# Turning the convolved x with VectorE and DRAM instead of TensorE, two output groups taken ahead, and four pairs of heads in one visit, in a Mamba-2 and attention trunk

## The chip, the cores and the metric

One core of one Trainium2 chip runs the whole program. The metric is the device time of one execution in microseconds (us), as the median over several executions. TensorE (PE) multiplies matrices into PSUM, VectorE (DVE) and ScalarE (ACT) work elementwise, GpSimd (POOL) and SyncE (SP) here only issue DMAs.

## What is computed

The reference is a decoder trunk of two layers on one sequence of 256 rows and 2,048 columns, all in float32:

```python
h = rmsnorm(x, a_norm_g);  proj = h @ w_in                      # 2048 x 10304
z, xbc, dt = split(proj);  xbc = silu(causal_conv(xbc))         # 4 taps
xs, B, C = split(xbc);     dt = softplus(dt + dt_bias);  a = -dt*exp(A_log)
# per group g of 8 (8 heads of 64 columns each), one chunk of 256 rows:
cb    = C[g] @ B[g].T
y     = (cb * exp(a_cum[l] - a_cum[s]) for s <= l) @ (xs*dt) + D*xs
y     = grouped_rmsnorm(y * silu(z), gnorm_g);  x = x + y @ w_out
kv    = rmsnorm(x, kv_norm_g) @ w_kv                            # K with rope, V
q, z  = split(rmsnorm(x, b_norm_g) @ b_w_in)
o     = causal_softmax_attention(rope(q), K, V) * silu(z)       # 16 heads, one block of 256
x     = rmsnorm(x + o @ b_w_out, final_norm_g)
```

## The kernel before

**Blocks and units.** Every weight matrix is cut into blocks of 512 columns. A block is worked in units of two k tiles (256 rows of weights, 512 KB). A unit is one load on SP's queue (`load`, L292), a split of the float32 weights into a rounded part `hi` on ACT and the rest `lo` on DVE (`split`, L311), and twelve PE products of 128x128 by 128x512 (`products`, L343): for each half of the 256 rows and each k tile, x_hi by hi, x_lo by hi and x_hi by lo. The split of a unit stands three units ahead of its products (`LOOK = 3`, with four raw buffers and five hi/lo buffers). `ORDER` (L34) is the sequence of the blocks of the first layer: B, C, x and z are blocks of `w_in`, `o0` to `o3` take the output columns 0 to 3 over the k tiles 0 to 7 (groups 0, 1), `o10` to `o13` over the k tiles 8 to 15 (groups 2, 3), and `p0` to `p3` over the k tiles 16 to 31 (groups 4 to 7).

**Side work.** Everything else is written as generators (`conv_gen`, `cb_gen`, `pair_gen`, `norm_gen`, `z_gen`, `x1_gen`, `att_gen` and others). While the program is recorded, `Side.some` (L154) is called between products; it gives a generator its next step when the modelled end of its last step lies `MARGIN` = 750 ns behind the modelled PE. So the place of each side instruction in each engine's queue is fixed ahead of time by a table of costs, and nothing is reordered while the program runs: each engine works through its queue in order.

**A group of the SSD layer.** An x block gives 256 rows by 512 channels with rows on the partitions. `turn` (L376) brings it to channels on the partitions: DVE transposes 32x32 blocks (tile `T`), SP writes `T` to DRAM, POOL reads it back in four pieces as `U`. `conv_gen` (L621) then runs the four taps, the bias and silu with channels on the partitions (tile `xs`). For the y product the rows must be on the partitions again, so PE transposes `xs` 128x128 at a time, in two sets of four per group, into a PSUM bank `s`, and DVE multiplies each set by dt into `xd` (L646 to L659). `pair_gen` (L692) makes, for each pair of heads, the decay `em` (POOL reads the cumulated decay rows from DRAM, ACT takes differences and the exponential, DVE multiplies by `cb`), and at every second pair PE runs the y products of two pairs (tile `s<-em,xd`, in float32, which the profile records as sixteen records a visit). DVE then adds D xs from PSUM into a separate tile `yt` and multiplies by the gate. `norm_gen` (L745) scales the group into the operand `yn[g]`.

**The turn to the second layer.** `out_evac` (L867) adds each output block to the residual. After the last block of a column, `x1_gen` (L847) lets PE transpose the new residual, four k tiles per block column, and ACT and DVE split each into `kvop`, the operand of the K and V blocks that follow at once. `r1_gen` (L883) makes the row norm and the scaled rope table `csr`. `open_b` (L821) closes the first layer's buffers. In the second layer `att_gen` turns the attention weights through DRAM in the same way, and its outputs become `oop`, the operand of the last four blocks.

Only these lines set the order around the change:

```python
if entry[2] <= PE.ns - MARGIN:                  # L161, Side.some
    most -= self.advance(entry)
ks = range(8 * (i // 10), 8 * (i // 10) + 8) if kind == "o" else range(16, 32)   # L930
if u == first_p + 12:                           # L1202
    open_b()
```

## Time and profile before

| | us |
|---|---|
| median of three executions | 1143.38 (1142.94 to 1145.92) |
| the profiled execution, its own time | 1143.61 |
| its span, first to last instruction | 1141.9 |
| PE busy | 1130.1 (99% of the span) |
| DVE busy | 839.2 (73%) |
| ACT busy | 641.6 (56%) |
| moved by DMA | 258.91 MB, 227 GB/s on average |
| mean granted clock of TensorE | 0.997 of full speed |

Busy time of PE is an upper bound of its use, since products are pipelined and overlap in the records; starts of consecutive instructions tell what each costs. Stages: the SSD stage with all blocks up to `o13` ends at about 582 us, `p0` to `p3` at 674, K and V at 850, the second layer's input blocks at 1043. All side work is recorded by one helper, L126, so instructions are told apart by their tiles. An operation that reads a wide tile shows the tile's name without its number.

### The profile page before, as it was taken

The page shows a single profiled execution, that of the slowest core. Times are in us where ns is not written, and L with a number is a line of the kernel's source. Part 1 is how long each engine was busy: PE and PEld are TensorE (multiplying, and loading weights), DVE is VectorE, ACT ScalarE, POOL GpSimd, SP SyncE. Part 2 cuts the span into 40 slices and gives each one's busy share as a digit, 9 for nine tenths or more (in the row PEclk, how much of TensorE's full clock was granted, in tenths as well). Part 3 has the DMA queues.
Part 4 walks back from the last instruction along what each step waited for, and adds up shares of the span by engine and source line. Part 5 has one row for each costly group of instructions (what it writes and reads, how often), then busy time and mean ns, then how long its engine had stood idle before and what let it go on. Part 6 is the DMA issues. An engine that isn't in the chain of part 4 may idle for free.

```text
span 1141.9 us, 14900 instructions
## 1 busy us (share of the span) xinstructions
PE 1130.1 (99%) x5217; PEld 923.2 (81%) x5217; DVE 839.2 (73%) x1283; ACT 641.6 (56%) x890; POOL 124.4 (11%) x217
## 2 busy tenths in 40 slices
PE   9999999999999999999999999999999999999996
PEld 6888888888888888888878888888888888888885
DVE  5787878778799878787877558876445597887564
ACT  5666566767656666667554655434343444445353
POOL 2011112012011111101000000000000012122000
PEclk9999999999999999999999999999999999999998
DMA  8787888878778777777765467768658688888852
GB/s 263 222 242 242 249 229 278 268 243 253 210 222 240 223 237 225 237 234 231 215 232 177 162 197 218 224 200 261 220 174 244 209 248 237 263 250 261 254 185 92
DMA packets 130363, 258.91 MB, mean 227 GB/s; under 512 B 12976, under 2 KB 13824, under 8 KB 129904
## 3 DMA queue, kind: packets, MB, share of 16 engines
q1 hardware_dynamic: 119232, 226.01, 63.2%
q0 software_dynamic: 11056, 31.95, 10.9%
q8 instruction: 41, 0.67, 0.2%
q14 instruction: 34, 0.28, 0.1%
HBM read 235.83 MB, written 22.09 MB: 226 GB/s over the span
## 4 chain that ended last, share of the span: by engine, by line
PE 96%; DMA 1%; DVE 1%; ACT 0%; SPq 0%; issue 0%; ACTq 0%; DVEq 0%
PE ps L126 90%; PE s L126 6%; DMA raw<-in_a_w_in_dram 1%; PE ps_dt L126 0%; DVE xs L126 0%; DVE lo L126 0%; ACT hi L126 0%; SPq L416 0%; DVE x L126 0%; DVE T L126 0%; SPq L306 0%; ACT T L126 0%; ACT x L126 0%; DVE sfin L126 0%; ACTq L1243 0%
## 5 line engine op out<-in xcount | busy, mean ns | idle before, releaser
L126 DVE TENSOR_TENSOR lo<-raw,hi 128x1024 fp32r<-128x1024 f32 (+1 forms) x385 | 462.7, 1215 | 192.1 <-ACT hi L126 189.1
L126 ACT ACTIVATE hi<-raw 128x1024 fp32r<-128x1024 f32 (+1 forms) x385 | 397.7, 1052 | 263.3 <-PE ps L126 137.5
L126 PE MATMUL ps<-hi,hT 128*128 128x512 f32 x1280 | 401.1, 394 | 0.5 <-ACT hi L126 0.4
L126 PEld LDWEIGHTS ps<-hi,hT 128*128 128x128 f32 x1280 | 235.6, 188 | 49.2 <-issue 2.1
L126 PE MATMUL ps<-lo,hT 128*128 128x512 f32 x640 | 249.8, 390 | 0.0
L126 PE MATMUL ps<-hi,bop 128*128 128x512 f32 x512 | 161.1, 396 | 0.0
L126 PE MATMUL ps<-hi,yn 128*128 128x512 f32 x512 | 159.7, 393 | 0.0
L126 PE MATMUL ps<-hi,kvop 128*128 128x512 f32 x512 | 158.2, 390 | 0.0
L397 POOL DMA_DIRECT2D U<-turned x128 | 74.3, 587 | 748.9 <-DMA turned<-T 408.2
L126 PEld LDWEIGHTS ps<-lo,hT 128*128 128x128 f32 x640 | 120.1, 188 | 26.4 <-DVE lo L126 0.9
L126 PEld LDWEIGHTS ps<-hi,kvop 128*128 128x128 f32 x512 | 95.7, 188 | 19.7
L126 PEld LDWEIGHTS ps<-hi,bop 128*128 128x128 f32 x512 | 95.8, 188 | 19.4
L126 PEld LDWEIGHTS ps<-hi,yn 128*128 128x128 f32 x512 | 94.7, 188 | 19.4 <-issue 0.5
L126 PE MATMUL ps<-lo,yn 128*128 128x512 f32 x256 | 99.8, 390 | 0.0
L126 PE MATMUL ps<-lo,bop 128*128 128x512 f32 x256 | 99.8, 390 | 0.0
L126 PE MATMUL ps<-lo,kvop 128*128 128x512 f32 x256 | 99.7, 389 | 0.0
L126 PE MATMUL ps<-hi,oop 128*128 128x512 f32 x256 | 78.9, 390 | 0.0
L126 DVE STREAM_TRANSPOSE T<-ps 128x512 f32<-128x512 f32 x64 | 43.4, 699 | 25.6 <-ACT ps L126 15.9
L126 DVE SCALAR_TENSOR_TENSOR xs<-u,cw,xs 128x255 f32<-128x255 f32 (+2 forms) x144 | 59.7, 475 | 0.0
L126 ACT ACTIVATE em<-em,dal 128x128 f32<-128x128 f32 (+1 forms) x128 | 54.4, 449 | 5.0 <-DMA em<-AC 2.9
L126 PEld LDWEIGHTS ps<-lo,bop 128*128 128x128 f32 x256 | 48.0, 188 | 10.3
L126 PEld LDWEIGHTS ps<-lo,yn 128*128 128x128 f32 x256 | 48.0, 188 | 10.1
(165 smaller groups left out, 922.5 us busy)
## 6 DMA issues: line engine op xcount, KB each, us to landing
raw<-in_a_w_in_dram SPq DMA_DIRECT2D x159, 512.0 KB, 5.3
raw<-in_a_w_out_dram SPq DMA_DIRECT2D x64, 512.0 KB, 4.8
raw<-in_w_kv_dram SPq DMA_DIRECT2D x64, 512.0 KB, 4.8
raw<-in_b_w_in_dram SPq DMA_DIRECT2D x64, 512.0 KB, 4.7
turned<-T SPq DMA_DIRECT2D x64, 256.0 KB, 4.3
U<-turned POOLq DMA_DIRECT2D x128, 128.0 KB, 6.5
raw<-in_b_w_out_dram SPq DMA_DIRECT2D x32, 512.0 KB, 4.9
em<-AC POOLq DMA_DIRECT2D x32, 256.0 KB, 6.0
```

What stands on the lines that cost most here:

```text
L126: return call(out, *args, **kw)
L397: POOL.dma_start(U[32 * q:32 * q + 32].rearrange("p (b c) -> p b c", b=8), src)
```

## The change

- `conv_gen` no longer lets PE transpose `xs`. After silu, DVE transposes 32x32 blocks of `xs` into `u` (two instructions a group), SP writes `u` to DRAM (`turned_x`, 512 KB), POOL reads it back into `u` in four pieces of 128 KB, and DVE multiplies by dt into `xd` in four instructions from SBUF.
- `pair_gen` is split: `em_gen` makes the decays one pair at a time, and `y_gen` runs the y products of all four pairs of a group in one visit into two PSUM banks. It writes y over `xs`, so `yt` goes; `xs` and `em` get four buffers each.
- `p0` to `p3` keep the k tiles 24 to 31 alone; new blocks `o20` to `o23` take the k tiles 16 to 23 (groups 4, 5) just ahead of them.
- A generator whose next step needs a PSUM bank `s`, that is one that will use PE, waits until it lies 3,000 ns behind the modelled PE instead of 750.
- The factor 0.5 of the gate moves into a row norm `r0h` that is halved once, the gate product becomes two plain multiplications a group, and the second layer takes q2 ahead of z1.

```diff
+MARGIN_PE = 3000.0
-ORDER = "... z7 o12 o13 p0 p1 p2 p3".split()
+ORDER = "... z7 o12 o13 o20 o21 o22 o23 p0 p1 p2 p3".split()
-        entry[2] = max([at] + [e.ns for e, b in zip(self.engines, before) if e.ns > b])
+        entry[2] = max([entry[2], at] + [e.ns for e, b in zip(self.engines, before) if e.ns > b])
-            if entry[2] <= PE.ns - MARGIN:
+            if entry[2] <= PE.ns - (MARGIN_PE if getattr(entry[1], "pe", False) else MARGIN):
-... "xs": ([P, 4, L], 3), ... "em": ([P, 2, 384], 2), ... "yt": ([P, 4, L], 2)})]
+... "xs": ([P, 4, L], 4), ... "em": ([P, 2, 384], 4), ...})]
+        ready.pe = "s" in tags                                       # can()
-        late(blocks[n_out], 8, 2)
+        late(blocks[n_out], 4, 2)
+        DVE.tensor_scalar(r0h, r0, 0.5, None, op0=OP.mult)           # first_norm
...
+        U = u.rearrange("p j l -> p (j l)")                          # conv_gen
+        for t in range(2):
+            DVE.transpose(U.rearrange("p (b t j l) -> p t b j l", b=4, t=2, j=4)[:, t],
+                          v[:, :, t * P:(t + 1) * P].rearrange("p j (b l) -> p b j l", b=4))
+        X = hbm.tile([P, 1024], F32, name="turned_x", tag=f"X{group % 2}")
+        SP.dma_start(X, U)
+        written = DVE.ns + WRITE
+        for b in range(4):
+            src = bass.AP(tensor=X.tensor, offset=X.offset + b * L, ap=[[1024, 32], [32 * 1024, 4], [1, L]])
+            POOL.dma_start(U[32 * b:32 * b + 32].rearrange("p (a c) -> p a c", a=4), src)
+        yield copied(U, written, 4 * 600.0)
         yield lambda: "dal" in st and can("xd")()
-        for i in (0, 2):
-            yield can("s")
-            p = take("s").rearrange("p (t c) -> p t c", t=2)
-            for e in range(2):
-                for t in range(2):
-                    PE.transpose(p[:, t, e * P:(e + 1) * P], v[:, i + e, t * P:(t + 1) * P], ident)
-            yield
-            DVE.tensor_mul(xd[...], p..., st["dal"][...])
+        for t in range(2):
+            for h in range(2):
+                DVE.tensor_mul(xd[:, t]..., U..., st["dal"][...])
...
+    def y_gen(g):
+        yield lambda: ("xd", g) in st and st.get(("ems", g)) == 4
+        yield max(when["xd", g], *(when["em", g, j] for j in range(4)))
+        yield can("s", "s")
+        for i in (0, 2):
+            q = take("s").rearrange("p (j l) -> p j l", j=2)
+            for j in (i, i + 1):
+                ...                                  # the four y products of pair j, as before
+        for i in (0, 2):
+            yield
+            for j in (i, i + 1):
+                DVE.scalar_tensor_tensor(y[:, j, :], y[:, j, :], Dv[:, c:c + 1], Q[i // 2][:, j - i, :], ...)
+        yield lambda: ("z", g) in st
+        for i in (0, 2):
+            DVE.tensor_mul(v, v, by_channel(z)[:, i:i + 2])
+            yield
...
-            ks = ... if kind == "o" else range(16, 32)
+            ks = ... if kind == "o" else range(24, 32)
-    for kind, n in ("z0", "q0", "q1", "z1", "q2", "q3", "z2", "z3"):
+    for kind, n in ("z0", "q0", "q1", "q2", "z1", "q3", "z2", "z3"):
-        if u == first_p + 12:
+        if u == first_p + 4:
```

The products of the blocks are as many as before, 4,608 and the 16 of dt. What moves on the engines is shown at three places. The first is **PE at group 4**. Before, two sets of four transposes of `xs` stand among the products of a block (`ps<-hi,hT`, `ps<-lo,hT`), and a visit holds two pairs (each pair is one row of 64x256 and one of 64x128):

```order
L126 MATMUL ps<-lo,hT 128x512
L126 MATMUL s<-ident,xs 128x128 x4
L126 MATMUL ps<-hi,hT 128x512 x2
...
L126 MATMUL s<-em,xd 64x256 x2
L126 MATMUL s<-em,xd 64x128 x2
L126 MATMUL s<-em,xd 64x256 x2
L126 MATMUL s<-em,xd 64x128 x2
```

With the change the group's one visit stands between two blocks:

```order
L127 MATMUL ps<-lo,yn_2257 128x512
L127 MATMUL s<-em,xd 64x256 x2
L127 MATMUL s<-em,xd 64x128 x2
L127 MATMUL s<-em,xd 64x256 x2
L127 MATMUL s<-em,xd 64x128 x2
L127 MATMUL s<-em,xd 64x256 x2
L127 MATMUL s<-em,xd 64x128 x2
L127 MATMUL s<-em,xd 64x256 x2
L127 MATMUL s<-em,xd 64x128 x2
L127 MATMUL ps<-hi,hT 128x512 x2
```

The transposes are gone from PE in all eight groups, 64 of them, and sixteen visits of two pairs have become eight of four.

The second is **DVE at group 4**, where `lo` is the rest of one unit's weights, `nt` the norm of an earlier group, and `T<-ps` the turn of the next block. Before, `xd` is made from the PSUM tile of the transposes:

```order
L126 TENSOR_TENSOR xd<-s,dal 128x2x256
L126 TENSOR_TENSOR em<-em,cb 128x768
L126 TENSOR_TENSOR nt_3298<-nt_3298 128x2
L126 TENSOR_TENSOR lo<-raw,hi 128x1024
L126 TENSOR_TENSOR nt_3298<-nt_3298 128x2
L126 SCALAR_TENSOR_TENSOR nt_3298<-nt_3298 128x2
L126 TENSOR_TENSOR xd<-s,dal 128x2x256
```

With the change `u` is turned, and `xd` comes seven splits later:

```order
L127 STREAM_TRANSPOSE u<-xs 128x4x128 x2
L127 TENSOR_TENSOR lo<-raw,hi 128x1024 x2
L127 TENSOR_TENSOR em<-em,cb 128x768
L127 TENSOR_TENSOR lo<-raw,hi 128x1024
L127 TENSOR_TENSOR em<-em,cb 128x768
L127 TENSOR_TENSOR lo<-raw,hi 128x1024
L127 SCALAR_TENSOR_TENSOR z<-z,U 128x1024
L127 STREAM_TRANSPOSE T<-ps 128x512 x2
L127 TENSOR_TENSOR lo<-raw,hi 128x1024 x3
L127 TENSOR_TENSOR xd<-u,dal 128x4x64 x4
```

Between the turn of `u` and its first use stand seven splits here, and six or seven in the other groups; the trip through DRAM lies beside them.

The third is **DVE at the first K block**, whose operand `kvop` is made from PE's last transposes of the residual; `r` is the norm's chain, `csr` the scaled rope table, which needs PE's transposes of `r`. Before, the last `kvop` (k tile 15) stands two splits ahead of `csr`:

```order
L126 SCALAR_TENSOR_TENSOR kvop<-s,gv,kvop 128x256
L126 TENSOR_TENSOR r_6034<-r_6034 128x2
L126 SCALAR_TENSOR_TENSOR r_6034<-r_6034 128x2
L126 TENSOR_TENSOR lo<-raw,hi 128x1024
L126 TENSOR_SCALAR r1h<-r_6034 128x2
L126 TENSOR_TENSOR lo<-raw,hi 128x1024
L126 TENSOR_TENSOR csr<-cs,rB 128x512
```

With the change it stands behind `csr` and a pair of `x1T`:

```order
L127 TENSOR_TENSOR lo<-raw,hi 128x1024
L127 TENSOR_TENSOR csr<-cs,rB 128x512
L127 SCALAR_TENSOR_TENSOR x1T_5634<-x1T_5634,gv,rB 128x256 x2
L127 SCALAR_TENSOR_TENSOR kvop<-s,gv,kvop 128x256
L127 TENSOR_TENSOR bop_6123<-x1T_5634,bop_6123 128x2x256
```

On PE the transposes of `r` now come ahead of the last ones of `x`, with six products between them. From the transposes of `x` to the first product of the k tile 15 PE has nine products left, and from those of `r` fifteen.

## Rows read from the trace of the kernel before

**Rows 1.** The page, part 4: the chain of work that ended last, its shares of the span by engine and by line.

```profile
PE 96%; DMA 1%; DVE 1%; ACT 0%; SPq 0%; issue 0%; ACTq 0%; DVEq 0%
PE ps L126 90%; PE s L126 6%; DMA raw<-in_a_w_in_dram 1%; PE ps_dt L126 0%; DVE xs L126 0%; DVE lo L126 0%; ACT hi L126 0%; SPq L416 0%; DVE x L126 0%; DVE T L126 0%; SPq L306 0%; ACT T L126 0%; ACT x L126 0%; DVE sfin L126 0%; ACTq L1243 0%
```

**Rows 2.** The waits of PE, all that the profile lists: engine, tile, line <- what was waited for; us in total, times, the longest.

```profile
PE s L126 <- DVE early L126: 1.2, 1, 1.2
PE s L126 <- DMA xl<-in_x_dram: 0.5, 1, 0.5
PE ps L126 <- ACT hi L126: 0.4, 1, 0.4
```

**Rows 3.** The chain in order of time, one piece of it, 1,008 products long: start, us, what.

```profile
689.20 228.51 PE ps L126 x1008
```

**Rows 4.** Busy time by stretch of the span, the two stretches of the SSD stage: us from the start, length, busy us of PE, PEld, DVE, ACT, POOL (with instructions), granted clock of TensorE, DMA share, GB/s.

```profile
100.00:340.00 240.00, 240.00 (x1145) 195.30 (x1144) 190.57 (x297) 161.20 (x219) 31.98 (x52) 1.00 0.82 246
340.00:582.00 242.00, 242.00 (x1165) 196.36 (x1164) 198.25 (x313) 157.60 (x212) 31.19 (x51) 1.00 0.77 230
```

**Rows 5.** Groups of instructions of PE: shapes, count | busy us, mean ns of one.

```profile
L126 PE MATMUL s<-em,xd 128*64 128x256 f32 (+1 forms) x256 | 24.3, 332 | 0.0
L126 PE MATMUL s<-ident,xs 128*128 128x128 f32 x64 | 9.6, 272 | 0.0
```

**Rows 6.** PE in order of time around one set of four transposes of x: start, us from the first start to the last end, engine, line, instruction, count.

```profile
232.41 0.60 PE L126 MATMUL s<-ident,xs 128*128 128x128 f32 x4
232.76 0.71 PE L126 MATMUL ps<-hi,hT 128*128 128x512 f32 x2
233.31 0.40 PE L126 MATMUL ps<-lo,hT 128*128 128x512 f32 x1
233.54 0.62 PE L126 MATMUL ps<-hi,hT 128*128 128x512 f32 x2
```

**Rows 7.** PE in order of time around one visit of two pairs (columns as above). Six products lie between the third row shown and the last.

```profile
139.76 0.39 PE L126 MATMUL ps<-lo,hT 128*128 128x512 f32 x1
140.08 1.52 PE L126 MATMUL s<-em,xd 128*64 128x256 f32 x16
141.53 0.73 PE L126 MATMUL ps<-hi,hT 128*128 128x512 f32 x2
...
143.02 0.62 PE L126 MATMUL ps<-hi,hT 128*128 128x512 f32 x2
```

**Rows 8.** PE, two cuts into that same visit: the first begins at the fifth of its sixteen records, the second at the thirteenth, which does for the second pair what the fifth does for the first.

```profile
140.56 1.04 PE L126 MATMUL s<-em,xd 128*64 128x128 f32 x12
141.21 0.39 PE L126 MATMUL s<-em,xd 128*64 128x128 f32 x4
```

**Rows 9.** PE in order of time at the first C B products of a group (tile s<-xs).

```profile
98.98 0.39 PE L126 MATMUL ps<-lo,hT 128*128 128x512 f32 x1
99.48 0.92 PE L126 MATMUL s<-xs 128*128 128x256 f32 x4
```

**Rows 10.** Groups of instructions of DVE, by shape: count | busy us, mean ns of one | idle time before them and what ended it.

```profile
L126 DVE TENSOR_TENSOR lo<-raw,hi 128x1024 fp32r<-128x1024 f32 x383 | 461.3, 1218 | 191.5 <-ACT hi L126 188.5 <-PE ps L126 2.0
L126 DVE STREAM_TRANSPOSE T<-ps 128x512 f32<-128x512 f32 x64 | 43.4, 699 | 25.6 <-ACT ps L126 15.9 <-DMA turned<-T 5.0 <-PE ps L126 4.6
L126 DVE TENSOR_TENSOR xd<-s,dal 128x512 f32<-128x512 f32 x16 | 10.9, 683 | 0.1
L126 DVE SCALAR_TENSOR_TENSOR yt<-yt,z 128x256 f32<-128x256 f32 x32 | 13.1, 419 | 0.2
L126 DVE TENSOR_TENSOR x<-ps,x 128x512 f32<-128x512 f32 x32 | 21.5, 686 | 18.4 <-PE ps L126 18.4
```

**Rows 11.** One turn through DRAM in order of time: its two transposes on DVE, its four reads issued by POOL, and the first reader of what came back, on ACT. In brackets the idle time before and what ended it.

```profile
85.52 1.30 DVE L126 STREAM_TRANSPOSE T<-ps 128x512 f32<-128x512 f32 x2
92.05 2.32 POOL L397 DMA_DIRECT2D U<-turned  x4 [9.38 <-DMA turned<-T]
100.47 1.06 ACT L126 ACTIVATE u<-U 128x1024 f32<-128x1024 f32 x1 [2.49 <-DMA U<-turned]
```

**Rows 12.** The two longest waits of ACT (us in total, times, the longest), and two lines of DMA issues: count, KB each, median us from issue to landing.

```profile
ACT hi L126 <- PE ps L126: 137.5, 93, 3.0
ACT hi L126 <- DMA raw<-in_a_w_in_dram: 49.7, 30, 3.8
turned<-T SPq DMA_DIRECT2D x64, 256.0 KB, 4.3
U<-turned POOLq DMA_DIRECT2D x128, 128.0 KB, 6.5
```

**Rows 13.** The first K products, in order of time: a kvop half on DVE, the transposes of the norm on PE, the scaled table csr and a pair of x1T on DVE.

```profile
686.09 0.48 DVE L126 SCALAR_TENSOR_TENSOR kvop<-s,gv,kvop 128x256 fp32r<-128x256 f32 x1
688.82 0.38 PE L126 MATMUL s<-ident,r 128*128 128x128 f32 x2
690.31 0.68 DVE L126 TENSOR_TENSOR csr<-cs,rB 128x512 f32<-128x512 f32 x1
690.91 0.87 DVE L126 SCALAR_TENSOR_TENSOR x1T<-x1T,gv,rB 128x256 f32<-128x256 f32 x2
```

**Rows 14.** The last attention output, in order of time: the product that follows its visit on PE, and the end of its operand on DVE.

```profile
1065.58 0.70 PE L126 MATMUL ps<-hi,oop 128*128 128x512 f32 x2
1068.37 0.68 DVE L126 TENSOR_TENSOR oop<-U,oop 128x512 fp32r<-128x512 f32 x1
```

More of the change, by code (lines that the diff above doesn't have):

```diff
@@ L31 @@
 MARGIN = 750.0
-ORDER = "B0 d0 C0 x0 z0 x1 z1 x2 z2 x3 z3 B1 o0 C1 o1 x4 o2 z4 x5 o3 z5 x6 o10 z6 x7 o11 z7 o12 o13 p0 p1 p2 p3".split()
+MARGIN_PE = 3000.0
+ORDER = "B0 d0 C0 x0 z0 x1 z1 x2 z2 x3 z3 B1 o0 C1 o1 x4 o2 z4 x5 o3 z5 x6 o10 z6 x7 o11 z7 o12 o13 o20 o21 o22 o23 p0 p1 p2 p3".split()
 LOAD = 4700.0
@@ L224, in can, with ready @@
     def can(*tags):
-        return lambda: all(of(t).free(t) > 0 for t in tags)
+        def ready():
+            return all(of(t).free(t) >= tags.count(t) for t in tags)
+        ready.pe = "s" in tags
+        return ready
     def take(tag):
@@ L709, in pair_gen @@
         st["em", g, j], when["em", g, j] = E, clock.last
-        if j % 2:
-            yield lambda: ("xd", g) in st and ("em", g, j - 1) in st
-            yield max(when["xd", g], when["em", g, j - 1])
-            yield lambda: of("s").free("s") > 1 and (("y", g) in st or can("yt")())
-            for i in (j - 1, j):
-                xd, E, q = st["xd", g], st.pop(("em", g, i)), take("s")[:, :L]
+        st["ems", g] = st.get(("ems", g), 0) + 1
+        if st["ems", g] == 4:
+            give(st["cb", g])
@@ L724, in pair_gen @@
-            if ("y", g) not in st:
-                st["y", g], st["n", g] = take("yt"), 0
+        give(xd)
+        for i in (0, 2):
             yield
-        else:
-            yield lambda: ("q", g, j) in st
-            yield when["q", g, j]
-        xd, xs, q = st["xd", g], st["xs", g], st.pop(("q", g, j))
-        y = st["y", g][:, j, :]
-        DVE.scalar_tensor_tensor(y, xs[:, j, :], Dv[:, c:c + 1], q, op0=OP.mult, op1=OP.add)
-        give(q)
-        st["x", g] = st.get(("x", g), 0) + 1
@@ L741, in pair_gen @@
-        st["n", g] += 1
-        if st["n", g] == 4 and g not in (1, 3):
+        for i in (0, 2):
+            v = y[:, i:i + 2, :].rearrange("p j (b l) -> p j b l", l=32)
+            DVE.tensor_mul(v, v, by_channel(z)[:, i:i + 2])
+            yield
+        st["y", g] = y
+        st["n", g] = 4
+        if g not in (1, 3):
             give(z)
@@ L791, in z_gen @@
             z = take("z")
-        ACT.activation(z, U, AF.Tanh, scale=0.5)
+        ACT.activation(z, U, AF.Tanh)
         yield
@@ L799, in evac @@
         def evac(ps, t):
-            U, there = turn(ps, t, r0)
+            U, there = turn(ps, t, r0h)
             if t:
@@ L812, in evac @@
             for j in range(4):
-                side.add(pair_gen(g, j), lambda: "AC" in st and can("em")())
+                side.add(em_gen(g, j), lambda: "AC" in st and can("em")())
+            side.add(y_gen(g))
             side.add(norm_gen(g), lambda: st.get(("n", g)) == 4)
@@ L929, in trunk_kernel @@
             n = i % 10
-            ks = range(8 * (i // 10), 8 * (i // 10) + 8) if kind == "o" else range(16, 32)
+            ks = range(8 * (i // 10), 8 * (i // 10) + 8) if kind == "o" else range(24, 32)
             if name == "p0":
@@ L1048, in att_gen @@
         yield
-        if ("z", h0) not in st:
+        if ("gate", h0) not in st:
             yield can("q")
@@ L1054, in att_gen @@
             o = z
-            yield lambda: ("z", h0) in st
-        gate = st.pop(("z", h0))
+            yield lambda: ("gate", h0) in st
+        gate = st.pop(("gate", h0))
         DVE.tensor_mul(gate.heads, in_32s(o), gate.heads)
@@ L1082, in gate_gen @@
         for i, half in enumerate(two(U)):
-            st["z", 4 * n + 2 * i] = half
+            st["gate", 4 * n + 2 * i] = half
     def zb_evac(n):
```

41 lines of the change are left out of this document (22 added, 19 removed).

## The prediction

> **What bounds it.** I read the chain of work that ended last first. PE carries 96% of it: 90% products of weight blocks (`ps`) and 6% side work (`s`) [rows 1]. Then the waits of PE: three in the whole span, 2.1 us together, all at the start [rows 2]. So PE hardly ever stands still, and the time is the sum of what its instructions cost. A product costs what the longest clean piece of the chain shows: 228.51 us for 1,008, that is 0.227 us [rows 3]. The 4,624 products of both kernels take 1,048 us at that price, and the rest of PE's time is mostly side visits. The other engines have room even in the SSD stage: in 482 us DVE is busy 389 us (81%) and the 16 DMA engines 0.77 to 0.82, at a full clock [rows 4]. ACT waits longer for PE to free a split buffer (137.5 us) than for weights of the first layer (49.7 us) [rows 12], which says that the splits run ahead of PE as far as their buffers let them. A PE instruction that goes is therefore worth its own cost, as long as nothing new makes PE wait.
>
> **The transposes of x.** Sixty-four leave PE [rows 5]. Their busy time of 9.6 us is not their price, since records overlap, so I take starts. Four start at 232.41, three products follow, and the next one starts at 233.54: 1.13 us, of which three products are 0.68 [rows 6]. A set costs 0.45 us, and sixteen sets 7.2 us. All of it lies on PE's path.
>
> **Four pairs a visit.** The y products stay, the switches between products and side work halve. After the product at 139.76 the next would have started at 139.99; the visit and six products end at 143.02. That is 3.03 us, less 6 x 0.227 = 1.36: a visit of two pairs costs 1.67 us [rows 7]. Inside it the second pair follows the first by 141.21 - 140.56 = 0.65 us [rows 8]. Two pairs are 1.30, so entering and leaving costs 0.37. Eight visits fewer give 8 x 0.37 = 3.0 us. The least that it can give is nothing, if two pairs that now share a PSUM bank hold each other up. I take 3.0: the step of 0.65 that I measured crosses from one bank to another, and the four products of a pair share a bank already and fill that step between them.
>
> **The wider margin.** There is almost nothing for it to win, because PE does not wait for its side operands [rows 2]. One place is visible: before the first C B products PE starts 0.50 us after its last product instead of 0.23 [rows 9]. With the change they stand one split later in its queue, so I count 0.3 us won. Elsewhere I count nothing.
>
> **What is added.** On DVE a group gets two transposes (0.70 each, as `T`, which reads PSUM), and four multiplications of 256 elements (0.42, as the gate's) take the place of two of 512 (0.68); the gate goes the other way, from four of 0.42 to two of 0.68. That is 1.4 us a group, 11.2 in all, and `o20` to `o23` bring eight more additions of 0.69, 5.5 us [rows 10]. These 17 us cost nothing while DVE keeps a fifth of its time free; that cover gone, each would delay a split. The halved norm is one instruction on two columns a partition. DMA gets 8 x 2 x 512 KB = 8.4 MB on 258.9, which at 238 GB/s, the mean of the two stretches, is 7% of what the SSD stage moves: its share goes from 0.80 to about 0.86. On SP the write of `turned_x` stands between weight loads and waits for DVE's transposes, on POOL its reads wait for that write; behind them wait weight loads for units further ahead on SP, and the reads of z and of `em` on POOL.
>
> **The trip through DRAM** is the one new wait on DVE: `xd` stands there with splits queued behind it. The same kind of trip now runs from the end of `T` at 86.82 to the arrival at 100.47, 13.7 us [rows 11]. Six or seven splits stand between, one per unit of 12 x 0.227 = 2.72 us, so at least 16.3 us. I count nothing; at worst PE waits when the splits' lead of three units, 8.2 us, is gone too, which takes a trip of 24.5 us. The Trainium skill (VectorE: DVE Perf Modes, The three transpose paths) says that a plain copy whose access pattern does the transposing is 19 times slower than the hardware's transpose when the innermost stride is large, and it sends a 128x128 transpose to TensorE. That speaks against this change; the rows are on the other side, since reads of this kind land in 6.5 us [rows 12] and each piece they move is a contiguous run.
>
> **Output blocks and second layer.** No product is added or removed. PE waited neither at `p0` nor in the attention, so the longer cover of group 7 and the other order of q2 and z1 win nothing [rows 2]. Two places get tighter. At the first K block the last `kvop` is made behind `csr`: `csr` begins 1.49 us after PE's transposes of the norm (a split lies in between, as it does with the change), then come 0.68, 0.87 and 0.48, 3.5 us [rows 13]. PE has 15 products and two visits of two transposes, about half of 0.45 each, until it reads it: 3.9 us. If that split starts late by all its 1.22 us, PE waits 0.8; so the place costs 0 to 0.8, and I take 0.3. The last attention output now has 21 products, 4.8 us, from its visit to its use; now it takes from 1065.58 to 1069.05, 3.5 us [rows 14]. Nothing.
>
> **Sum.** -7.2 - 3.0 - 0.3 + 0.3 = -10.2 us on the profiled execution's 1143.61, that is 1133.4; the median of the runs is 0.23 us lower, so I forecast **1133.2 us**.
>
> **Rivals.** First, *the tight places take a part back*: the joined visit saves nothing (+3.0), and a split of 1.22 stands late at both tight places (+2.4): 1138.6 us. For it: four decays and two banks must now be ready at once, and both places have under 1.5 us in hand. Against it: em and xs have twice and four thirds the buffers, and the margin is four times as wide.
>
> Second, *the weights become the bound*. If the DMA engines can't pass the 0.82 that the busiest stretch shows [rows 4], the SSD stage must grow by 0.86/0.82, some 5% of 482 us, 24 us; if half of the 8.4 MB finds gaps, 12 us, which eats the gain: 1145 us, no change. Against it: the waits for weights are a third of the waits for PE.
>
> Third, on the other side, *the trip is late*. DVE stands at `xd`, the splits behind it are late, and PE waits once a group. From 24.5 us on each microsecond costs eight; it is slower than before by more than 0.3% from 24.5 + (10.2 + 3.4)/8 = 26.2 us on, twice the 13.7 of the rows, and a trip of 28 us gives 8 x 3.5 - 10.2 = +18: 1161 us. For it: two kinds of trip now share POOL's queue, where one write that is late holds all reads behind it. Against it: 13.7 us included a POOL that had waited 9.38 us for the write alone [rows 11]. By the skill's factor of 19 this rival would be the forecast; no row bears that factor out.
>
> **How the numbers follow.** The forecast has a chance of 0.78, the first rival 0.13, the second 0.05, the third 0.04. About 0.3%, 3.4 us, can be told from no change, so faster means below 1140.0. The first two cases are faster, 0.91; the second rival is no change, 0.05; the third slower, 0.04. The range runs from 1131.5 (the sum without the K block's 0.3 is 1132.9, and the runs of before scatter by more than a microsecond around their median) to 1139.5, which takes in a joined visit without gain, the K block at 0.8 and the first rival with a microsecond of scatter.
>
> **What would show it.** Right: no `s<-ident,xs` on PE; the y products in eight visits of thirty-two records, each costing 1.67 + 1.30, about 2.97 us; `s` at about 5% of the chain; PE's waits still under some 3 us; DVE busy some 856 us; 267 MB moved. Wrong: waits of PE for `lo`, `kvop` or `oop`; DVE waiting for `u<-turned_x` by more than a few us a group; a lower granted clock.

## The result, and the profile after

| | before | forecast | after |
|---|---|---|---|
| median, us | 1143.89 (1142.94 to 1145.92) | 1133.2 (1131.5 to 1139.5) | 1158.76 (1156.22 to 1163.08) |
| profiled execution, us | 1143.61 | 1133.4 | 1159.48 |
| DVE busy, us | 839.2 | 856 | 850.4 |
| moved by DMA, MB | 258.91 | 267 | 267.29 |

The ratio of after to before is 1.0131, with an interval of 1.0097 to 1.0166: slower by 15 us (before was run beside it), where I had given faster 0.91. The work went as forecast: no `s<-ident,xs` is left, and a visit of four pairs costs what the sum said. This is PE around one that nothing disturbs, columns as in rows 7; five products lie between its second and third row:

```profile
418.71 0.39 PE L127 MATMUL ps<-lo,yn 128*128 128x512 f32 x1
419.03 2.82 PE L127 MATMUL s<-em,xd 128*64 128x256 f32 x32
...
423.04 0.39 PE L127 MATMUL ps<-lo,hT 128*128 128x512 f32 x1
```

423.04 - 418.71 - 6 x 0.227 = 2.97 us, as forecast. But PE, which had stood still for 2.1 us [rows 2], now does so for 18.8 us in all, where I had given under 3. The chain by engine and line (to [rows 1]) shows how much of the end is set elsewhere:

```profile
PE 53%; DVE 16%; DMA 15%; ACT 9%; issue 6%; POOL 1%; ACTq 0%; SPq 0%; DVEq 0%; POOLq 0%
PE ps L127 49%; DVE lo L127 7%; DMA raw<-in_a_w_in_dram 6%; ACT hi L127 5%; PE s L127 4%; DVE xs L127 3%; DMA raw<-in_w_kv_dram 2%; DMA turned<-T 2%; DMA Es<-turned_E 2%; DMA raw<-in_a_w_out_dram 1%; DVE T L127 1%; ACT em L127 1%; DMA U<-turned 1%; ACT xs L127 1%; ACT u L127 1%
```

The longest waits of PE (to [rows 2]):

```profile
PE s L127 <- issue: 4.2, 2, 2.8
PE s L127 <- DMA Es<-turned_E: 3.7, 2, 2.7
PE ps L127 <- DVE lo L127: 2.2, 4, 0.7
PE s L127 <- DVE r L127: 1.9, 1, 1.9
PE s L127 <- DVE nt L127: 1.9, 3, 0.8
PE ps L127 <- DVE kvop L127: 1.8, 1, 1.8
```

To have one measure for all kernels I took every start-to-start step of PE, subtracted what that pair of instructions takes when nothing waits, and added up what is over by more than 0.06 us. It takes in waits and the slow clock behind them. It is read from the one profiled execution of each kernel, which lies up to 6 us from its median (1164.76 and 1158.68 us in the run without `o20` to `o23`), and a sum falls up to 3.4 us short of what that execution's time asks for. So a difference of 2 or 3 us between two kernels says little. **Lost time of PE by stretch**, us (the stretch limits are those of the profile before; in the slower kernels the stages end later than that):

| kernel | 100 to 582 (SSD) | 582 to 674 (p blocks) | 674 to 850 (K, V) | from 850 |
|---|---|---|---|---|
| before | 0.1 | 0 | 0 | 1.4 |
| after | 11.0 | 2.4 | 5.3 | 7.0 |

That is 24.2 us more than before; with the 10.2 saved and the 15.9 by which the profiled execution is longer, 26.1 were to be found, and some 2 us lie in steps too small to be counted.

**In the SSD stage** the two windows of [rows 4] read after the change:

```profile
100.00:340.00 240.00, 233.34 (x1093) 187.84 (x1094) 192.73 (x303) 157.95 (x218) 39.54 (x66) 0.99 0.88 257
340.00:582.00 242.00, 241.01 (x1129) 197.18 (x1127) 192.20 (x298) 159.13 (x217) 36.71 (x60) 1.00 0.83 247
```

The place of the first y visit shows what happens. Windows of before, same columns:

```profile
136.00:142.00 6.00, 6.00 (x39) 4.53 (x38) 4.16 (x7) 1.83 (x2) 2.80 (x5) 1.00 0.91 252
142.00:148.00 6.00, 6.00 (x28) 4.94 (x27) 3.03 (x4) 1.76 (x2) 0.94 (x2) 1.00 1.03 265
148.00:152.00 4.00, 4.00 (x19) 3.32 (x18) 0.54 (x1) 3.97 (x7) 0.00 (x0) 1.00 0.59 216
```

and of after, with one more behind it:

```profile
136.00:142.00 6.00, 6.00 (x28) 4.99 (x27) 5.42 (x7) 2.35 (x3) 2.20 (x4) 1.00 1.02 340
142.00:148.00 6.00, 4.98 (x22) 3.78 (x21) 0.73 (x1) 0.99 (x1) 2.33 (x4) 1.00 1.05 228
148.00:152.00 4.00, 2.24 (x16) 1.66 (x18) 3.70 (x6) 1.12 (x2) 0.51 (x1) 0.87 0.97 230
...
151.00:155.00 4.00, 4.00 (x27) 3.08 (x24) 0.80 (x1) 1.06 (x2) 2.17 (x3) 0.58 0.89 249
```

The DMA share, 0.82 on average, touched 1.03 here before the change too; now it is about 1 for sixteen us, with the four reads of `turned_x` (issued from 136.84 on) among weight loads and a turn. What suffers is the landing of the weights. The weight loads of 125 to 150 us (count, KB, median us to landing), first before, then after:

```profile
raw<-in_a_w_in_dram SPq DMA_DIRECT2D x9, 512.0 KB, 6.6
```

```profile
raw<-in_a_w_in_dram SPq DMA_DIRECT2D x8, 512.0 KB, 9.1
```

So a split is late, and with it everything behind it on DVE. ACT, DVE and PE of after, in order of time, an extract of each (five products lie between the last two rows of PE):

```profile
147.01 1.06 ACT L127 ACTIVATE hi<-raw 128x1024 fp32r<-128x1024 f32 x1 [5.54 <-PE ps L127]
```

```profile
148.10 1.23 DVE L127 TENSOR_TENSOR lo<-raw,hi 128x1024 fp32r<-128x1024 f32 x1 [5.37 <-ACT hi L127]
149.24 1.43 DVE L127 TENSOR_TENSOR xd<-u,dal 128x256 f32<-128x256 f32 x4
```

```profile
146.60 0.39 PE L127 MATMUL ps<-lo,hT 128*128 128x512 f32 x1
149.76 5.03 PE L127 MATMUL s<-em,xd 128*64 128x256 f32 x32 [2.78 <-issue]
...
155.98 0.40 PE L127 MATMUL ps<-lo,hT 128*128 128x512 f32 x1
```

`u` was there, its last read having landed at 146.79; `xd` is late because the split ahead of it on DVE is. The profile puts ACT's idle time down to PE and PE's to "issue", the last releasers that it saw. The load of the weights that ACT splits at 147.01 tells more. It was issued at 135.34 and landed 11.6 us later, at 146.91. In a run with the same order and small transfers, told below, the same load was issued at 135.69 and took 6.4 us, and PE did not stop. The two loads (count, KB, us to landing), first after, then that run:

```profile
raw<-in_a_w_in_dram SPq DMA_DIRECT2D x1, 512.0 KB, 11.6
```

```profile
raw<-in_a_w_in_dram SPq DMA_DIRECT2D x1, 512.0 KB, 6.4
```

The visit then runs for most of its length at the lower of TensorE's two clocks, 1.2 GHz instead of 2.4 (granted clock 0.58 on average from 151 to 155 us, last window row).

**The trip itself** takes longer than the prediction's 13.7 us, and the place of `xd` is nearer than its 16.3. From the traces, us by group of the SSD layer, from the end of the turn of `u` on DVE to the landing of the last read, and to the first `xd`:

| group | 0 | 1 | 2 | 3 | 4 | 5 | 6 | 7 |
|---|---|---|---|---|---|---|---|---|
| after, trip | 14.9 | 20.1 | 15.0 | 16.8 | 15.1 | 18.2 | 17.5 | 19.0 |
| after, to `xd` | 17.4 | 20.7 | 16.7 | 19.1 | 15.3 | 18.8 | 17.7 | 19.2 |
| same order, small transfers, to `xd` | 12.3 | 20.7 | 14.8 | 17.0 | 13.7 | 17.6 | 15.0 | 16.4 |

With small transfers nothing on DVE waits for `u`, so the last row is about the room that the order gives. The trip of after is longer than that in groups 0, 2 and 4 to 7. At the first y visit a split in time would have brought `xd` forward by no more than 2.4 us, since `u` would then have held it until 146.79. The wait of DVE for `u` in all, and its longest, in group 6 (the turn of `u` and `xd`), after:

```profile
DVE xd L127 <- DMA u<-turned_x: 4.3, 3, 2.6
```

```profile
515.58 1.30 DVE L127 STREAM_TRANSPOSE u<-xs 128x512 f32<-128x512 f32 x2
...
534.55 1.43 DVE L127 TENSOR_TENSOR xd<-u,dal 128x256 f32<-128x256 f32 x4 [2.58 <-DMA u<-turned_x]
```

and the same two in the run with small transfers:

```profile
507.62 1.30 DVE L127 STREAM_TRANSPOSE u<-xs 128x512 f32<-128x512 f32 x2
...
523.89 1.43 DVE L127 TENSOR_TENSOR xd<-u,dal 128x256 f32<-128x256 f32 x4
```

**At the first K block** `r` itself is late, and `kvop` behind a split that is late too. DVE of after, to [rows 13]:

```profile
693.71 0.16 DVE L127 TENSOR_REDUCE r<-ss 128x2 f32<-128x8 f32 x1 [1.06 <-ACT T L127]
...
701.39 1.23 DVE L127 TENSOR_TENSOR lo<-raw,hi 128x1024 fp32r<-128x1024 f32 x1 [1.40 <-ACT hi L127]
702.53 0.69 DVE L127 TENSOR_TENSOR csr<-cs,rB 128x512 f32<-128x512 f32 x1
703.14 0.88 DVE L127 SCALAR_TENSOR_TENSOR x1T<-x1T,gv,rB 128x256 f32<-128x256 f32 x2
703.93 0.48 DVE L127 SCALAR_TENSOR_TENSOR kvop<-s,gv,kvop 128x256 fp32r<-128x256 f32 x1
```

PE transposes `r` at 698.38 after a wait of 1.9 us; `csr` follows 4.15 us later, not 1.49.

### The profile page after: what moved, and what is told of

It is laid out like the page before. It is cut to its first block, busy times and chain, and to the rows that moved or that the text cites. A ratio compares the mean times of both kernels' runs of the same rounds, so it can differ in the third digit from the quotient of the medians.

```text
span 1157.8 us, 14848 instructions
## 1 busy us (share of the span) xinstructions
PE 1129.2 (98%) x5153; PEld 920.1 (79%) x5153; DVE 850.4 (73%) x1308; ACT 638.6 (55%) x889; POOL 142.9 (12%) x249
## 2 busy tenths in 40 slices
DMA packets 133050, 267.29 MB, mean 231 GB/s; under 512 B 13616, under 2 KB 14464, under 8 KB 132592
## 4 chain that ended last, share of the span: by engine, by line
PE 53%; DVE 16%; DMA 15%; ACT 9%; issue 6%; POOL 1%; ACTq 0%; SPq 0%; DVEq 0%; POOLq 0%
PE ps L127 49%; DVE lo L127 7%; DMA raw<-in_a_w_in_dram 6%; ACT hi L127 5%; PE s L127 4%; DVE xs L127 3%; DMA raw<-in_w_kv_dram 2%; DMA turned<-T 2%; DMA Es<-turned_E 2%; DMA raw<-in_a_w_out_dram 1%; DVE T L127 1%; ACT em L127 1%; DMA U<-turned 1%; ACT xs L127 1%; ACT u L127 1%
## 5 line engine op out<-in xcount | busy, mean ns | idle before, releaser
L127 PEld LDWEIGHTS ps<-lo,kvop 128*128 128x128 f32 x256 | 48.1, 188 | 11.1 <-DVE lo L127 1.1
L127 PEld LDWEIGHTS ps<-hi,oop 128*128 128x128 f32 x256 | 48.6, 191 | 10.0
```

What stands on the lines that cost most here:

```text
L127: return call(out, *args, **kw)
```

## The experiments

The four figures in brackets behind each result are the lost time by stretch, in the order of the columns of the table above. Each ratio is to the kernel before, run beside it.

### Single parts put back into the changed kernel

```diff
-MARGIN_PE = 3000.0
+MARGIN_PE = 750.0
```

> The changed kernel with one number put back: steps that need a PSUM bank s wait for 750 ns behind the modelled PE again, not 3,000. The trace of the changed kernel (1158.8 us) shows PE waiting at some twenty places. Theory M (the wider margin puts PE's side steps too near to, or past, the products that need their results): the waits for r and kvop at the first K block (2.1 + 1.9 us) and for Es in the attention (1.2 + 2.8 us, and about 3 us of half clock behind the second) go, some 11 us, so about 1148 us. Theory X (the trip of x through DRAM is what makes weights, splits and decays late): these waits lie in the SSD stage, about 16 us there with the half clock at 150 us, and stay; with the second layer as it is, 1157 to 1161 us. Theory O (the shorter p blocks and the order of the second layer's blocks make those places tight, whatever the margin): 1157 to 1161 us as well.

1157.94 us, ratio 1.0123 (1.0100 to 1.0145) [7.6, 0.6, 7.3, 6.3]. Not clearly faster: theory M alone falls. PE no longer waits for `kvop`, but it waits 3.2 us for the residual at the transposes of x.

```diff
 # conv_gen: the lines of before again, four transposes by PE into s, xd from s; give(u) after silu
-        SP.dma_start(X, U)
+                    PE.transpose(p[:, t, e * P:(e + 1) * P], v[:, i + e, t * P:(t + 1) * P], ident)
```

> The changed kernel with PE's 64 transposes of x back and the trip of x through DRAM gone; margin, blocks, joined visits and the rest as in the changed kernel. The transposes cost PE 7.2 us (16 sets of 0.45). Theory X: some 16 us of waits and half clock in the SSD stage go with the trip, so 1158.8 + 7.2 - 16 = 1150 us, and the DMA share between 100 and 340 us falls from 0.88 to about 0.82. Theory M or O alone: the SSD stage's waits stay, 1158.8 + 7.2 = 1166 us. With both halves true it is between 1150 and 1156 us.

1154.10 us, ratio 1.0082 (1.0067 to 1.0098) [2.2, 0, 5.4, 4.6]. PE works 7.2 us more, and the program is 0.0049 of the time, 5.6 us, shorter than with the whole change: here the trip cost more than it gave. The intervals of the two ratios just touch, so the 5.6 can be anything from 1 to 10 us, and the order is drawn anew. The DMA share between 100 and 340 us is 0.83, as forecast, and the losses from K on stay.

```diff
-... o12 o13 o20 o21 o22 o23 p0 p1 p2 p3
+... o12 o13 p0 p1 p2 p3          # p over range(16, 32), late(..., 8, 2), first_p + 12
```

> The changed kernel without the blocks o20 to o23: p0 to p3 take the k tiles 16 to 31 again, with eight units each. Theory O: the waits for r and kvop at the first K block, 2.1 + 1.9 us, go, because the transposes of the residual have eight units a block instead of four; group 7 has less cover, but before that was enough: about 1154.5 us, and 8 additions fewer on DVE. Theory M: the two waits stay, since the margin sets them: 1158 to 1160 us. Theory X says nothing of these places: 1158 to 1160 us.

1158.68 us, ratio 1.0129 (1.0112 to 1.0145) [15.7, 7.6, 1.2, 5.3]. The waits for `r` and `kvop` are gone, as theory O said, but PE now waits for `yn` of group 7, and the SSD stage, whose order is drawn anew, loses more, so the forecast of 1154.5 us failed.

```diff
-"z0", "q0", "q1", "q2", "z1", "q3", "z2", "z3"
+"z0", "q0", "q1", "z1", "q2", "q3", "z2", "z3"
```

> The changed kernel with the second layer's blocks in their old order (z1 ahead of q2). Theory O: the wait for Es at 1054 us (2.8 us) and the 3 us of half clock behind it go, perhaps the 1.2 us at 998 us too: 1152 to 1153 us. Theory M: the margin, not the order, makes the attention's last steps late, and a wait of the same kind stays: 1157 to 1160 us.

1160.84 us, ratio 1.0145 (1.0117 to 1.0174) [13.7, 1.1, 8.1, 5.1]. No gain; PE does not wait for `Es`, but for `oop` (1.6 us, with slow clock behind).

### Single parts on the kernel before

The parts of change are the ones shown in the diff of the change; each stands alone here.

> The kernel before with one part of the change: x is turned by VectorE and through DRAM, PE's 64 transposes of it go; visits of two pairs, margin, blocks and order as before. Theory X (the trip makes weights, splits and decays late): 7.2 us are saved on PE and some 16 us of waits and half clock come in the SSD stage, 1152 to 1154 us, with PE waits for lo, hi, em, nt or squares between 100 and 582 us and none behind. Theory N (the trip is hidden, as the prediction had it, and the loss needs the other parts): 1136 to 1138 us.

1192.78 us, ratio 1.0423 (1.0396 to 1.0450) [38.0, 18.3, 0, 1.4]. Far worse than either theory. PE around `yn` of group 3:

```profile
288.37 1.55 PE L126 MATMUL s<-em,xd 128*64 128x256 f32 x8 [4.34 <-DVE xs L126]
295.75 0.66 PE L126 MATMUL s<-ident,nt 128*128 128x128 f32 x2 [5.83 <-DVE nt L126]
307.66 1.55 PE L126 MATMUL s<-em,xd 128*64 128x256 f32 x8 [11.25 <-DVE em L126]
310.20 1.55 PE L126 MATMUL s<-em,xd 128*64 128x256 f32 x8 [0.99 <-PE s L126]
```

These steps stand in PE's queue with no product between them: when an output block came up, its group was not ready, and the program records what is missing back to back (`force`). The trip lengthens the way from an x block to `yn` beyond the cover that the blocks give.

```diff
+        SP.dma_start(X, u)                           # before, behind silu; POOL reads X back into u,
+        POOL.dma_start(U2[32 * b:32 * b + 32], src)   # x4; nothing reads u, PE transposes xs as before
```

> The kernel before, with the same 512 KB written to DRAM and read back in four pieces per group into u, at the same place and through the same queues, which nothing reads; PE's transposes and xd stay as before. What it adds is the traffic, its places in SP's and POOL's queues and the longer hold on u; it lacks DVE's transposes of u and DVE's wait at xd. If the traffic is what makes the weights late: PE waits for lo and hi in the SSD stage as in the changed kernel, 1150 to 1158 us, and the DMA share between 100 and 340 us rises from 0.82 to about 0.88. If the harm is DVE's wait and added work at u and xd: 1143 to 1145 us.

1164.28 us, ratio 1.0175 (1.0155 to 1.0196) [3.4, 16.3, 0, 1.4]. Slower, but not where expected: `u` is held longer, the order is drawn anew, and group 7 stands without cover at 607 us (PE idle 11.8 for `nt`). Since its order changed, it does not answer its question; the same-order runs below do.

> The kernel before, with steps that take a bank s held until they lie 3,000 ns behind the modelled PE, instead of 750 (the two-pair visit, which asks for its banks in another way, keeps 750). Theory M (the wider margin alone pushes PE's side steps into the products that need them): waits for r, kvop and Es, 4 to 11 us, so 1148 to 1155 us. Otherwise, with two-thirds of the waits due to the trip: 1143 to 1145 us.

1167.89 us, ratio 1.0206 (1.0182 to 1.0230) [2.5, 15.7, 0.1, 7.2]. More than either theory gave. The wider margin alone uncovers group 7 too, and costs the attention 5.8 us more than before.

```diff
 # the changed kernel with PE's transposes, MARGIN_PE = 750, no o20 to o23, z1 ahead of q2
```

> The changed kernel with four parts put back: PE transposes x, the margin is 750 ns, no o20 to o23, the old order in the second layer. What is left of the change is the joined visit with its buffers, y over xs, and the gate as two multiplications. If eight visits fewer are worth what the prediction said (8 x 0.37 us), and the waits belong to the other parts: 1141 us. If the joined visit itself makes PE wait (four decays, the norm of the group later): 1144 us or more, with waits for em, nt or squares in the SSD stage.

1150.90 us, ratio 1.0058 (1.0039 to 1.0078) [3.8, 0, 2.0, 4.0]. The eight visits cost 2.97 us each where nothing disturbs them, so the 3.0 us are won, and some 10 lost. From the first K product on, PE, DVE, ACT and the queues of POOL and SP have row for row the order of before, and 4.6 us more are lost even there; why, these runs do not show.

> The kernel before with o20 to o23 ahead of p0 to p3, which keep the k tiles 24 to 31; nothing else. If the shorter p blocks make the first K block tight by themselves: waits for r and kvop of 2 to 4 us there, 1145 to 1148 us. If those waits of the changed kernel need its wider margin too: 1143 to 1145 us.

1150.63 us, ratio 1.0063 (1.0049 to 1.0077) [1.0, 0.6, 8.6, 1.9]. Slower than either forecast; the blocks need no help from the margin. PE waits at the first K block for the last addition to the residual `x`, and at 694.82 another 2.28 us for `r`:

```profile
678.91 0.30 PE L126 MATMUL s<-ident,x 128*128 128x128 f32 x1 [2.25 <-DVE x L126]
679.81 0.33 PE L126 MATMUL s<-ident,x 128*128 128x128 f32 x1 [0.60 <-DVE x L126]
```

The transposes of the last residual column stand ahead of its addition's end. Behind the wait for `r` products follow at the slow clock (0.72 on average from 694 to 700 us).

> The trip of x through DRAM on the kernel before (1192.8 us alone, where PE stood 8 to 16 us each in visits of group 3 at 288 to 314 us, and of groups 6 and 7 at 607 to 665 us, with no products left to put between them) and now the blocks o20 to o23 with it. If these blocks are the cover that the longer way to yn needs: the losses at 607 to 665 us go, some 25 us, and the one at 300 us stays: 1160 to 1170 us. If they are no cover: 1185 us or more.

1182.89 us, ratio 1.0337 (1.0324 to 1.0350) [37.2, 1.4, 7.8, 2.3]. Between the two forecasts, but both parts can be told apart: the blocks take away 16.9 us between 582 and 674 and bring 7.8 in K and V.

### The same order, other transfers

In these runs PE, DVE and ACT have instruction for instruction the order of the kernel that they start from.

```diff
-        SP.dma_start(X, U)
+        SP.dma_start(X[0:32, 0:256], U[0:32, 0:256])
-            POOL.dma_start(U[32 * b:32 * b + 32]..., src)
+            POOL.dma_start(U[0:32, 64 * b:64 * b + 64], X[0:32, 64 * b:64 * b + 64])
```

> The changed kernel with the order on TensorE, VectorE and ScalarE kept instruction for instruction; only the trip's data shrink. Per group 32 KB instead of 512 KB are written to DRAM, and as much read back, in four small reads, so most of u is not turned across partitions (the y product is left with wrong rows). In the changed kernel PE loses 11 us to waits and half clock between 100 and 582 us, 2.4 us from there to 674, 5.3 in K and V, 7.0 in the second layer. Theory D (the trip's bytes delay weights, decays and turns): most of the 11 us goes, 1147 to 1150 us. Theory P (the order itself is at fault, drawn up by a table that knows none of these waits): 1155 to 1160 us.

1148.55 us, ratio 1.0050 (1.0031 to 1.0070) [6.1, 0, 7.2, 2.4]: 0.0081 x 1144 = 9.3 us below the changed kernel, 5 to 14 by the intervals of the two ratios. Against the changed kernel the SSD stage loses 4.9 us less, the p blocks 2.4 less, K and V 1.9 more. The second layer loses 4.6 less, though no trip of `u` runs there; why, these runs do not show. Small transfers also make the trip shorter, so this run does not part what the trip's bytes do to others from what its length does to `xd`. The place of above on DVE, in this run:

```profile
143.34 1.22 DVE L127 TENSOR_TENSOR lo<-raw,hi 128x1024 fp32r<-128x1024 f32 x1 [0.80 <-ACT hi L127]
144.48 1.42 DVE L127 TENSOR_TENSOR xd<-u,dal 128x256 f32<-128x256 f32 x4
```

and its windows:

```profile
142.00:148.00 6.00, 6.00 (x28) 4.76 (x26) 4.24 (x7) 2.13 (x2) 1.68 (x3) 1.00 0.95 226
148.00:152.00 4.00, 4.00 (x38) 2.99 (x38) 0.00 (x0) 0.01 (x1) 2.71 (x4) 1.00 1.05 260
```

`xd` stands 4.8 us earlier, PE does not stop, and the weight loads of 125 to 150 us land in 6.3 us, not 9.1. The share is hardly lower, so it is not the share that tells; I take it that what counts is what the DMA engines carry when a weight is wanted.

```diff
+        SP.dma_start(X, v.rearrange("p j l -> p (j l)"))        # before, behind silu
+        for b in range(4):
+            POOL.dma_start(X2[32 * b:32 * b + 32], X[32 * b:32 * b + 32])
```

> The kernel before with the order on TensorE, VectorE and ScalarE kept instruction for instruction; per group xs (512 KB) is also written to DRAM by SP's queue and copied back, within DRAM, in four pieces by POOL's queue, and nothing reads it. Theory D: waits for lo, hi, em and nt come in the SSD stage without any change of order, 8 to 12 us, 1152 to 1156 us. Theory P: 1143 to 1146 us.

1154.24 us, ratio 1.0098 (1.0083 to 1.0113) [8.3, 0, 0, 1.4]: 11 us for transfers that nothing reads. POOL of before:

```profile
171.06 1.42 POOL L698 DMA_DIRECT2D em<-AC  x2 [6.54 <-issue]
185.33 2.33 POOL L397 DMA_DIRECT2D U<-turned  x4 [12.86 <-DMA turned<-T]
```

and POOL and ACT of this run:

```profile
177.56 1.99 POOL L650 DMA_DIRECT2D back_x<-turned_x  x4 [12.50 <-DMA turned_x<-xs]
179.55 1.48 POOL L703 DMA_DIRECT2D em<-AC  x2
```

```profile
186.47 1.78 ACT L126 ACTIVATE em<-em,dal 128x128 f32<-128x128 f32 x4 [6.34 <-DMA em<-AC]
```

The reads of `em` stand behind reads that wait for a write, go out 8.5 us later, and ACT stands at `em` with splits behind it. PE then waits 2.0 us for `em` (at 196.09) and 2.6 for `nt` (at 200.47), and the clock falls (0.66 on average from 201 to 206 us): some 7 of the 8.3 us lie between 180 and 210 us, at this one group.

```diff
-        POOL copies X back at once
+        later.append((X, X2))     # POOL copies it back behind the next two reads of em
```

> The kernel before with the added traffic of the run that kept its order (512 KB of xs written and copied back per group, 1154.2 us, +11), and one difference: POOL issues the copies back behind the next two reads of em instead of ahead of them. Bytes, issue count and the order on TensorE, VectorE, ScalarE and SP are the same. Theory Q (POOL's queue: reads of em and U stand behind reads that wait for a write): the loss goes, 1143 to 1146 us. Theory B (the bytes themselves delay the other transfers): 1151 to 1156 us.

1144.18 us, ratio 1.0002 (0.9991 to 1.0014) [0, 0, 1.5, 1.4]. The same bytes through the same queues at another place cost nothing that can be measured.

```diff
+        SP.dma_start(XB, v...)    # on top of the small trip: 512 KB out, and back behind the reads of em
```

> The changed kernel with the order on TensorE, VectorE and ScalarE kept and the trip's own data shrunk to 32 KB (1148.6 us with that alone; the y product is left with wrong rows); now the missing bytes are moved all the same: xs, 512 KB a group, goes to DRAM by SP's queue behind the small write, and is copied back by POOL's queue behind the group's reads of em; nothing waits for it. Theory Q: 1147 to 1151 us, as without the bytes. Theory B: 1155 to 1160 us, as in the changed kernel.

1151.25 us, ratio 1.0064 (1.0050 to 1.0078) [6.7, 0, 7.6, 5.0]. Just above the range of theory Q. Of the 9.3 us, some 7.7 stay away with the bytes back; nothing waits for these bytes, and the trip stays short.

```diff
-            POOL.dma_start(U[32 * b:32 * b + 32]..., src)     # at once
+            SP.dma_start(U[32 * b:32 * b + 32]..., src)       # before the next load once the write counts as landed
```

> The changed kernel, its order on TensorE, VectorE and ScalarE kept; the reads of turned_x are issued by SP's queue, some one or two weight loads after the write, when the table counts the write as landed, and no longer by POOL's queue at once. The trip keeps all its bytes. Theory Q (reads of U and em stand behind reads that wait for the write on POOL's queue): 1148 to 1152 us, the level of the run with small transfers. If SP's queue is no better a place (weight loads now stand behind the four reads): 1156 to 1162 us, with longer waits of ScalarE for raw weights.

1164.21 us, ratio 1.0162 (1.0138 to 1.0185) [12.6, 3.7, 6.0, 4.3]. No gain; slower than both forecasts, and ScalarE's waits for raw weights are not longer, as the second one had it (56.5 us between 100 and 582 us, 59.1 in the changed kernel). The run does not settle whether POOL's queue is the cause in the changed kernel, since it brings a wait of its own: DVE waits 10.6 us for `u`, not 4.3, and group 4's reads go out 4.9 us after the write has landed, not 0.6. The Trainium skill (DMA: Bandwidth & Descriptors, Issuing engines are not separate DMA queues) says that transfers of all issuing engines run on the same 16 DMA engines and interleave. By that rule the choice of queue does not free the engines; this run agrees, with weights of the first layer landing in 5.9 us and `em` in 8.1 (median, 100 to 582 us), against 5.9 and 8.3 in the changed kernel.

```diff
 # as above, and MARGIN_PE = 750, z1 ahead of q2
```

> As the run with the reads on SP's queue, and besides MARGIN_PE at 750 and z1 ahead of q2 again, which redraws the order. If the waits at the first K block and in the attention belong to those two: 5 to 9 us below the run with the reads on SP's queue alone, 1140 to 1146 us. If any order drawn with the joined visit and the trip has such waits: within 4 us of it.

1154.09 us, ratio 1.0079 (1.0062 to 1.0096) [10.2, 0.6, 9.6, 3.1]. Ten us below the run before, more than the first theory's 5 to 9, but by the lost time only 1 of them in the second layer and none in K and V: the order was drawn anew, and no cause can be read from the difference.

### Is it only a redrawn order, or its table?

```diff
-MARGIN = 750.0
+MARGIN = 800.0                # before
```

> The kernel before with MARGIN at 800 ns in place of 750. Nothing is added or taken away; some side instructions stand a split or a product elsewhere. Theory P (the order of the kernel before is one of few without waits, and any redrawn order has some): 1148 to 1153 us, as the joined visit alone had it (1150.9). If the waits need a cause of their own in the change: 1143 to 1145 us.

1143.37 us, ratio 0.9999 (0.9990 to 1.0008) [0, 0, 0.3, 1.4]. A redrawn order needs no loss; theory P falls in its plain form.

```diff
-LOAD = 4700.0
+LOAD = 5900.0                 # after
```

> The changed kernel, and the table that draws up the order counts 5,900 ns from the issue of a weight load to its landing, the median that the changed kernel's trace shows, instead of 4,700. If the waits come from this figure being short: half of the 11 us between 100 and 582 us goes, 1150 to 1154 us. If it only redraws the order, with other waits: 1155 to 1163 us.

1159.19 us, ratio 1.0152 (1.0130 to 1.0174) [12.1, 0, 4.6, 7.7]. That figure of the table is not the cause.

No kernel here beats the one before.

## Why the prediction was wrong

- **Right:** the costs of what leaves PE. The transposes are gone, an undisturbed visit costs 2.97 us as forecast, DVE is 6 us below its forecast, the bytes are as forecast. What failed is the condition set at the start, that nothing new makes PE wait.
- **Wrong, the step that failed most: "The trip through DRAM ... I count nothing."** Cutting the trip down to 32 KB with the order held fixed takes away 9.3 us. Both numbers of the step were off. The trip took 14.9 to 20.1 us, not 13.7: the 13.7 were read from a single turn, at 85 to 100 us. And six or seven splits between the turn and `xd` are not 16.3 us: six splits enclose only five unit times, 13.6 us, and where nothing held `xd` up it came after 12.3 to 15.0 us in four groups of eight. DVE waits only 4.3 us for `u` all the same, since what stands ahead of `xd` on DVE was late too, as the split at the first y visit. The step also did not ask what the trip's transfers do to others while they run. The paragraph on what is added named the queue behind the writes and the reads of `em`, and gave it no price.
- **The second rival** came nearest in its mechanism, 12 us in the SSD stage through late weights, but for a reason that the runs contradict: the share did pass 0.82, and the run with the copies behind `em` moves as many bytes between 100 and 582 us (122.8 MB, 121.4 in the changed kernel) for nothing. What costs, where the runs show it, is transfers that stand ahead of a weight or of `em` when these are wanted. I gave it 0.05.
- **The first K block, 0.3 us, bound 0.8:** mis-sized; 5.3 in K and V. My bound started from PE's transposes of `r` as if these came on time, and PE waited 1.9 us for `r`. All eleven kernels with `o20` to `o23` lose 4.6 to 9.6 us in K and V, all others at most 2.0.
- **The wider margin, "elsewhere I count nothing":** alone it costs 24 us, 15.7 in the p blocks and 5.8 in the attention. In the changed kernel, which has `o20` to `o23`, taking it back gains nothing clear (1.0123 against 1.0131). I read [rows 2] as "nothing to win" and did not ask what a step held back longer loses. Of the 0.3 us at the first C B products nothing came either: they start 0.48 us after the product ahead of them (99.56 and 100.04), not 0.23.
- **"The longer cover of group 7 wins nothing":** true of the kernel before, wrong with the trip; without the blocks the trip loses 18.3 us there.
- **The third rival**, with a chance of 0.04, came nearest in number, 1161 us for 1158.76, by luck: it needed a trip of 28 us and DVE at `xd` in every group, and DVE stood there three times, 4.3 us in all. The rule of the Trainium skill named beside it (VectorE: DVE Perf Modes, Rules for kernel authors) sends a 128x128 transpose to TensorE, and the run that did so was faster by 0.0049 of the time, 5.6 us. Its factor of 19 (The three transpose paths) is for a copy with a large innermost stride, and no run here has one: each piece moved is a contiguous run of 1 KB, and the reads land in 7.1 us.
- **Four pairs a visit, "the least that it can give is nothing":** the joined visit with its buffers and the new gate is 6.9 us slower alone than before, though the 3.0 us are won. The prediction had no term for waits that it brings, other than the first rival's.
- **Open:** what loses these some 10 us of the joined visit; whether in the changed kernel the trip's transfers at their place or its length holds most of the 7.7 us that stay away when the bytes come later; and what the order of q2 and z1 does, which was not tried on the kernel before. The parts do not add: alone the trip costs 49 us, the margin 24, the joined visit 7 and the blocks 7, together with the new order of q2 and z1 15.

## What to carry to other kernels

A mean DMA share of 0.8 does not say that a transfer fits: look where it will stand (here windows of 6 us were at 1.03), at how weights land in the 25 us around it and at what stands behind it in the issuing queue, above all behind a read that waits for a write. Where the bounding engine has no waits, an instruction taken from it is worth its cost only while every operand on the new path is still early. Count that lead from the order itself: n instructions between two points enclose n - 1 of their steps. Price each place with under 2 us in hand. Try the parts of such a change one by one and with the order held fixed, since parts that redraw an order do not add.

## What the runs showed of the hardware that I had not expected

- At the first y visit PE stood still for 2.8 us, and its clock then fell: granted 0.58 on average from 151 to 155 us, for most of it the lower level, 1.2 GHz, and 2.4 GHz again from 155 us on. By starts the visit costs 155.98 - 146.60 - 6 x 0.227 = 8.02 us instead of 2.97; 2.85 of the 5.05 us are the wait, the other 2.2 the slow clock. Not every such wait is followed by it: with the blocks alone PE waited 2.25 us at 678.91, and the clock stayed full until another wait, of 2.28 us, at 694.82.
- A DMA share of 1.0 says little of the bytes: 340 GB/s at 1.02 from 136 to 142 us, 228 at 1.05 in the next six.
- The place in POOL's queue decided what the same transfers cost: 512 KB a group written and copied back took 11 us where the copies stood ahead of two reads of `em`, and nothing that can be measured behind them (1154.24 and 1144.18 us).
